# A head's four maximum blocks at 0.5 of a plan position, in place of 0.65 and 0.64

## The chip, the cores and the metric

The kernel runs on one core of one Trainium2 chip. The metric is the device time of one execution in microseconds, the median of the runs shown. Beside it stands one execution under the hardware profiler; all rows of the profile come from that one.

The engines are PE (TensorE, the matmuls), PEld (its weight loads), DVE (VectorE), ACT (ScalarE), POOL (GpSimd) and SP (SyncE, which issues transfers). Each engine works through its own instructions in the order in which the program lists them.

## What is computed

The reference is a trunk of two layers on 512 tokens of width 1024. One layer is, cut to what matters:

```python
h = rms_norm(x, attn_norm_g[l])
proj = h @ w_in[l]
c_q, c_kv, k_rope, gq, gk, gv, pool_in, gate_logits = split_columns(proj, IN_SIZES)
o_mla = mla_branch(c_q, c_kv, k_rope, ...)      # 8 heads, q and k 96 wide, v 64
o_gqa = gqa_branch(gq, gk, gv, ...)             # 8 heads on 2 k/v heads, 64 wide
o_pool = pool_branch(pool_in, ...)
merged = sum of sigmoid(gate) * (o @ w_branch) over the three branches
x = x + merged @ w_out[l]
x = x + (silu(u_gate) * u_val) @ ffn_w_down[l]  # u: conv of rms_norm(x) @ ffn_w_up
```

Both attentions are full softmax attentions over the 512 tokens:

```python
sc = jnp.einsum('bqgrd,bkgd->bgrqk', qi, k) * scale
p = jax.nn.softmax(sc, axis=-1)
```

## The kernel before

**Precision.** Every float32 operand of a matmul is split into a high and a low part, and a product is three matmuls (`mm3`, L534). A unit of weight work, as it is called here, is usually one such triple: 128 by 128 weights against 512 tokens.

**Order of a layer.** The input projection comes first, then the gqa attention, then the mla attention, then the output projection and the MLP. While an attention runs, PE has other work too: the gates of a branch (`feat_major` with the normalised input `HH`, `HL`) and the projections of the branches. They come as units from a `Filler` (L185), a generator that is stepped between the attention's steps. Beside gqa stand the units of the pool branch, the mla projections and the first of the gqa branch; beside mla the rest of the gqa branch and the first of the mla branch.

**One head of an attention** (`attention`, L1275). The head's keys and queries are turned and split (`t_q`, `t_k`, and `go_turn` for the trip through device memory that turns them). Then, step by step:

- `s_max(h, b)`, four times (b = 0 to 3; L1358): one matmul writes a block of 128 queries by 512 keys into the bank `ps_S`; DVE takes the negative maximum of each query into a column of `nm` (L314 in the profile). `ps_S` has one buffer, so the next block's matmul has to come after the reduction of the one before it. After the fourth block a transfer issued on ACT's queue (`row`, L1372) writes the 512 maxima as one row into the head's queries, `qb` in gqa and `qa` in mla.
- `probs(h, k)`, four times (L1379): 128 keys by 512 queries of scores into `ps_ST` or `ps_mi`. The row is one more line of the contraction, so that the maxima are already taken off. Then ACT takes the exponential, ACT or DVE makes the high part `ph`, DVE the low part `pl`, and a last step gathers `vt`.
- `av_hi`, `av_lo` (four each) and `av_rest`: the products with the values, in `ps_AV`.

**The plan.** The order of all these steps is made when the program is written out. Each step gets a position; a head is four positions, and head h starts at 4(h - 1). From `PLAN` come, in this order, the offsets of the turn, of `t_q`, of `t_k`, of the first `s_max`, the distance between two `s_max` blocks, the offsets of `av_hi` and `av_lo`, and the position at which the units shall be used up:

```python
tt, tq, tk, s0, ds, ah, al, end = PLAN[kind]
for h in range(8):
    p0 = 4.0 * (h - 1)
    ...
    for k in range(4):
        plan += [(p0 + s0 + ds * k, s_max, (h, k)), (p0 + 4 + k, probs, (h, k)),
                 (p0 + 4 + k + ah, av_hi, (h, k)), (p0 + 4 + k + al, av_lo, (h, k))]
```

The steps are sorted by position (a tie keeps the order of the list). Before each step, units are issued until their share fits the position:

```python
fill.upto(min(target, fill.total - spare))
while fill.done < min(target + SLACK, fill.total - spare) and waiting(fn, *args) and fill.step():
    pass
fn(*args)
```

`target` grows evenly with the position; positions below zero count PRO = 0.47 of their distance (`stretch`). `waiting` asks a clock (`Clock`, L208, and `Engine`, L279) that is advanced with assumed costs as instructions are listed: whether the step's inputs are ready and a bank is free. As long as they are not, up to SLACK = 35 units are issued ahead of their share. Among the assumed costs are 0.07 + 0.00105 us an element for a DVE reduction, 0.15 us for a signal between engines (SEM), and D_ROW = 3.4 us from the fourth reduction until the row of maxima has landed. `pick` (L506) uses the same clock to give a subtraction to DVE or POOL. The clock only sets the order: on the chip each engine goes on as soon as its semaphores allow.

Of the kernel before, what the change touches and what calls it, by code (L numbers as in the profile page):

```python
# [49 lines left out]
END = object()  # L50
RSQRT_BITS = 1597463007.0
SLACK = 35
PLAN = {"gqa": (-4.2, -1.0, -0.2, 0.0, 0.65, 2.411, 4.57, 32.003),
        "mla": (-6.2, -2.9, -1.0, 0.1, 0.64, 1.678, 1.82, 35.5)}

D_ROW, D_OUT, D_IN, D_LAT = 3.4, 3.2, 4.0, 6.0
D_SUM, D_FIRST = 2.0, (2.4, 2.4, 2.0, 2.4)
# [280 lines left out]
def trunk(ctx: ExitStack, tc: tile.TileContext, x, w, prm, gb, cst, out):  # L338
# [344 lines left out]
    def layer(l, sq, xsrc):  # L683
# [591 lines left out]
        def attention(kind, fill, okey, odst):  # L1275
# [218 lines left out]
            plan = []  # L1494
            tt, tq, tk, s0, ds, ah, al, end = PLAN[kind]
            for h in range(8):
# [514 lines left out]
```

## Time and profile before

| | us |
|---|---|
| median of 3 runs | 1546.02 |
| lowest, highest | 1543.15, 1547.62 |
| profiled execution | 1545.53 |
| its span, first to last instruction | 1543.7 |

| engine | busy us | share of the span |
|---|---|---|
| PE | 1536.6 | 100% |
| PEld | 1342.3 | 87% |
| DVE | 1171.0 | 76% |
| ACT | 1072.6 | 69% |
| POOL | 771.0 | 50% |

The first blocks of `ps_S` for gqa run at about 107 us and those for mla at about 237; in the second layer they run at 873 and 1003. A row of the profile gives a line of the kernel, an engine, an operation, the tiles as written<-read, the shape, and a count; in a list of groups the busy time and the mean duration in ns follow, in a timeline the start and the duration in us, with the idle time of the engine before it in brackets and what ended it. A tile's answer gives durations as minimum/median/maximum in ns, and the waits in us with their number.

### The profile page before, as it was taken

How to read it: one execution, taken by the hardware profiler on the slowest of the kernel's cores; microseconds unless marked ns; L12 is line 12 of the kernel's file. 1: busy time of each engine (PE TensorE's matmuls, PEld its weight loads, DVE VectorE, ACT ScalarE, POOL GpSimd, SP SyncE). 2: the span in 40 equal slices, each digit the busy share in tenths (PEclk: the TensorE clock that was granted, in tenths of full speed). 3: DMA queues.
4: the chain of work that ended last, by engine and by line, in shares of the span. 5: the costliest groups of instructions: out<-in, count | busy, mean ns of one | idle time of the engine just before them, and what ended most of it. 6: DMA issues, size and time to landing. Idle time of an engine off the chain costs nothing.

```text
span 1543.7 us, 24550 instructions
## 1 busy us (share of the span) xinstructions
PE 1536.6 (100%) x8337; PEld 1342.3 (87%) x8337; DVE 1171.0 (76%) x1960; ACT 1072.6 (69%) x2008; POOL 771.0 (50%) x828
## 2 busy tenths in 40 slices
PE   9999999999999999999999999999999999999999
PEld 8888888888889999999898888878888899999997
DVE  6877886776688888888756688768666888888885
ACT  5557875877677877786544587758766677777772
POOL 3984887753452222232488648766535522222222
PEclk9999999999999999999999999999999999999999
DMA  5432344658978888877435323546599778788763
GB/s 204 121 122 83 85 127 141 161 130 199 223 186 194 182 184 186 191 173 161 138 116 138 118 75 87 133 133 169 123 214 222 188 182 192 178 187 193 177 140 109
DMA packets 139517, 241.79 MB, mean 157 GB/s; under 512 B 30976, under 2 KB 53504, under 8 KB 139392
## 3 DMA queue, kind: packets, MB, share of 16 engines
q1 hardware_dynamic: 91872, 162.93, 33.6%
q0 software_dynamic: 42624, 77.09, 29.2%
q8 instruction: 65, 1.06, 0.3%
q10 hardware_dynamic: 4896, 0.21, 0.2%
q14 instruction: 60, 0.49, 0.1%
HBM read 149.41 MB, written 13.63 MB: 106 GB/s over the span
## 4 chain that ended last, share of the span: by engine, by line
PE 96%; DVE 2%; DMA 1%; ACT 0%; issue 0%; SPq 0%; ACTq 0%
PE ps_acc L526 41%; PE ps_AV L526 18%; PE ps_ST L526 16%; PE ps_S L526 10%; PE ps_mi L526 10%; DVE sq L306 1%; DMA qa<-nm 0%; DMA XM<-x 0%; DMA qb<-nm 0%; DVE ctl L310 0%; DVE rp L306 0%; ACT wh L299 0%; DVE gqr L306 0%; DVE ssr L314 0%; DVE ka L322 0%
## 5 line engine op out<-in xcount | busy, mean ns | idle before, releaser
L438 POOL DMA_DIRECT2D wl<-raw x188 | 170.3, 911 | 384.9 <-ACT wl L299 185.7
L299 ACT ACTIVATE wh<-raw 128x512 fp32r<-128x512 f32 (+2 forms) x449 | 264.9, 605 | 59.2 <-DVE raw L306 14.7
L306 POOL TENSOR_TENSOR wl<-raw,wh 128x512 fp32r<-128x512 f32 (+2 forms) x169 | 214.5, 1278 | 166.5 <-ACT wh L299 159.2
L438 POOL DMA_DIRECT2D fl<-raw x108 | 94.7, 876 | 166.8 <-ACT fl L299 68.6
L526 PE MATMUL ps_acc<-HH,wh 128*128 128x512 f32 x400 | 156.7, 392 | 0.4 <-DVE XM L310 0.4
L526 PE MATMUL ps_acc<-HH,wl 128*128 128x512 f32 x400 | 156.3, 391 | 0.0
L526 PE MATMUL ps_acc<-HL,wh 128*128 128x512 f32 x400 | 156.3, 391 | 0.0
L310 DVE SCALAR_TENSOR_TENSOR a<-u,prm,a 128x511 f32<-128x511 f32 x176 | 134.6, 768 | 18.9 <-ACT a L299 18.4
L314 DVE TENSOR_REDUCE nm<-ps_S 128x1 fp32r<-128x512 f32 x128 | 87.9, 686 | 46.3 <-PE ps_S L526 45.1
L299 ACT ACTIVATE wl<-wh 128x512 fp32r<-128x512 f32 (+1 forms) x188 | 118.1, 628 | 6.0
L299 ACT ACTIVATE a<-u,prm 128x512 f32<-128x512 f32 x88 | 71.2, 811 | 55.8 <-DVE u L306 55.7
L526 PE MATMUL ps_acc<-tf,wh 128*128 128x256 f32 x576 | 106.2, 282 | 0.0
L526 PEld LDWEIGHTS ps_acc<-tf,wh 128*128 128x128 f32 x576 | 94.3, 191 | 6.0
L526 PEld LDWEIGHTS ps_acc<-HH,wl 128*128 128x128 f32 x400 | 75.1, 188 | 16.3
L526 PEld LDWEIGHTS ps_acc<-HH,wh 128*128 128x128 f32 x400 | 75.3, 188 | 15.5 <-issue 0.7
L526 PEld LDWEIGHTS ps_acc<-HL,wh 128*128 128x128 f32 x400 | 75.2, 188 | 15.4
L526 PE MATMUL ps_acc<-tf,wl 128*128 128x256 f32 x288 | 81.5, 283 | 0.0
L306 DVE TENSOR_TENSOR wl<-raw,wh 128x512 fp32r<-128x512 f32 (+1 forms) x93 | 66.1, 711 | 17.6 <-ACT wh L299 17.3
L526 PE MATMUL ps_AV<-HH,wl 128*128 128x256 f32 (+1 forms) x240 | 78.2, 326 | 0.0
L526 PE MATMUL ps_AV<-HL,wh 128*128 128x256 f32 (+1 forms) x240 | 78.1, 326 | 0.0
L526 PE MATMUL ps_AV<-HH,wh 128*128 128x256 f32 (+1 forms) x240 | 78.1, 326 | 0.0
L306 DVE TENSOR_TENSOR pl<-ps_ST,ph 128x512 fp32r<-128x512 f32 x86 | 58.4, 683 | 17.1 <-ACT ph L299 13.6
(427 smaller groups left out, 5039.8 us busy)
## 6 DMA issues: line engine op xcount, KB each, us to landing
raw<-w SPq DMA_DIRECT2D x153, 512.0 KB, 4.0
wl<-raw POOLq DMA_DIRECT2D x184, 256.0 KB, 4.2
raw<-w SPq DMA_DIRECT2D x151, 256.0 KB, 3.7
fl<-raw POOLq DMA_DIRECT2D x108, 256.0 KB, 4.9
raw<-w SPq DMA_DIRECT2D x13, 384.0 KB, 3.0
XM<-x SPq DMA_DIRECT2D x16, 256.0 KB, 4.7
dtq<-tr SPq DMA_DIRECT2D x16, 192.0 KB, 2.0
dtk<-tr SPq DMA_DIRECT2D x16, 192.0 KB, 3.2
```

Of the source, the lines that this page charges most:

```text
L299: return self.eng.activation(out, in_, func, **k)
L306: return self.eng.tensor_tensor(out, *a)
L310: return self.eng.scalar_tensor_tensor(out, *a)
L314: return self.eng.tensor_reduce(out, in_, *a, **k)
L438: nc.gpsimd.dma_start(f(lo), r, accum_op=ALU.add)
L526: PE.matmul(o, lhsT=lhsT, rhs=rhs, start=start, stop=stop, skip_group_check=again)
```

## The change

The distance between two `s_max` blocks of a head becomes 0.5 positions in both attentions. Nothing else differs in the text of the kernel. The blocks b = 1, 2, 3 stand at 0.5, 1.0 and 1.5 positions behind the first in place of 0.65, 1.3 and 1.95 (gqa) and 0.64, 1.28 and 1.92 (mla). In gqa the third block of a head then has the position of the second `probs` of the head before it, and stands behind it.

```diff
 SLACK = 35
-PLAN = {"gqa": (-4.2, -1.0, -0.2, 0.0, 0.65, 2.411, 4.57, 32.003),
-        "mla": (-6.2, -2.9, -1.0, 0.1, 0.64, 1.678, 1.82, 35.5)}
+PLAN = {"gqa": (-4.2, -1.0, -0.2, 0.0, 0.5, 2.411, 4.57, 32.003),
+        "mla": (-6.2, -2.9, -1.0, 0.1, 0.5, 1.678, 1.82, 35.5)}
```

## The prediction

> **What bounds the kernel now.** I read the page's first part, its chain, and then the busy time in the four stretches in which the two attentions of the two layers run.
>
> ```profile
> span 1543.7 us, 24550 instructions
> PE 1536.6 (100%) x8337; PEld 1342.3 (87%) x8337; DVE 1171.0 (76%) x1960; ACT 1072.6 (69%) x2008; POOL 771.0 (50%) x828
> ...
> PE 96%; DVE 2%; DMA 1%; ACT 0%; issue 0%; SPq 0%; ACTq 0%
> ...
> 100.00:232.00 132.00, 132.00 (x604) 110.37 (x603) 101.58 (x186) 98.17 (x185) 92.36 (x117) 1.00 0.36 102
> 232.00:355.00 123.00, 123.00 (x536) 102.01 (x534) 89.22 (x146) 89.15 (x160) 77.93 (x76) 1.00 0.54 142
> 866.00:1000.00 134.00, 133.93 (x612) 111.98 (x611) 103.42 (x189) 100.04 (x188) 91.24 (x116) 1.00 0.35 98
> 1000.00:1124.00 124.00, 122.64 (x533) 101.30 (x532) 88.26 (x144) 88.88 (x160) 77.62 (x76) 1.00 0.56 142
> ```
>
> The reader is to see that PE has work all the time, in the attentions too (the columns are PE, PEld, DVE, ACT, POOL busy, then the clock, 1.00 throughout). In both gqa stretches DVE has 77% (101.58 of 132, 103.42 of 134), in both mla stretches 71 to 73%, so DVE is next. The change removes no matmul. What it can win is therefore only time in which PE waits, and what it can lose is new waits of PE. Busy time hides short waits, because a matmul's recorded end overlaps the next one's start; they are seen in the distance from start to start. That distance, undisturbed, is 5.44/24 = 0.227 us:
>
> ```profile
> 388.26 5.44 PE ps_ST L526 x24
> ```
>
> **The maxima, as they run now.** Two answers: the tile `nm`, and who waited for whom.
>
> ```profile
> L314 DVE TENSOR_REDUCE nm<-ps_S x128: 671/691/693, 108.2 to 1106.3; 128x1 fp32r<-128x512 f32 x128
> L1373 ACTq DMA_DIRECT2D qb<-nm x16: 476/477/554, 114.1 to 975.1; - x16
> L1373 ACTq DMA_DIRECT2D qa<-nm x16: 476/477/505, 245.5 to 1107.6; - x16
> ...
>   PEld ps_mi L526: 1.8, 1
> ...
>   PEld ps_ST L526: 0.9, 3
> ...
> DMA to landing us min/median/max: 1.9/1.9/5.8
> ...
> DVE nm L314 <- PE ps_S L526: 45.1, 57, 2.1
> ...
> PEld ps_S L526 <- POOL qa L306: 0.9, 3, 0.3
> ...
> PEld ps_S L526 <- DVE nm L314: 0.5, 2, 0.3
> ```
>
> There are 128 blocks of scores in `ps_S` (4 a head, 8 heads, 2 attentions, 2 layers), each with one matmul and one reduction of about 0.69 us, and 32 rows. PE's waits for a row are 1.8 + 0.9 = 2.7 us in the whole run. Most of it is one row, that of mla's first head in the second layer:
>
> ```profile
> 1011.79 5.81 DMA qa<-nm
> ...
> 1017.65 0.50 PE ps_mi L526
> ```
>
> It takes 5.81 us where the median is 1.9, and the scores that need it start when it lands. Of the 128 reductions 57 found DVE idle and waited for PE; the other 71 found DVE at work. That is the line that matters below, as `ps_S` has one bank: the next block's matmul cannot start before the reduction has read the bank.
>
> **What the edit moves.** A head is four positions of the plan. Its length in time, from the first scores of head 0 to those of head 7:
>
> ```profile
> 118.69 0.39 PE L526 MATMUL ps_ST<-qa,ka 128*128 128x512 f32 x1
> ...
> 212.56 0.39 PE L526 MATMUL ps_ST<-qa,ka 128*128 128x512 f32 x1
> ...
> 249.34 0.40 PE L526 MATMUL ps_mi<-qa,kl 96*128 96x512 f32 x1
> ...
> 343.58 0.40 PE L526 MATMUL ps_ST<-qa,kl 96*128 96x512 f32 x1
> ```
>
> (212.56 - 118.69)/7 = 13.41 us a head in gqa, 3.35 a position; (343.58 - 249.34)/7 = 13.46 in mla, 3.37 a position. Blocks 1, 2 and 3 of every head move up: in gqa by 0.15, 0.30 and 0.45 positions, in mla by 0.14, 0.28 and 0.42. So 96 matmuls, 96 reductions on DVE and 32 row transfers on ACT's queue stand sooner, the row by up to 0.45 x 3.35 = 1.5 us (mla 1.4; about half in head 0, whose positions are shrunk by PRO). Nothing is added or removed. They pass units of weight work (three matmuls each, 3 x 0.227 = 0.68 us) and some `av` matmuls on PE, evacuations on DVE, and exponentials and casts on ACT. No SP or POOL instruction belongs to the step. The matmuls cost nothing in another place. The row's issue takes 0.48 us on ACT's queue as before; if its reduction is late, the exponentials behind it wait, but ACT has 98.17 busy of 132, so I charge zero, and up to 0.7 (one reduction) a row if that room is gone.
>
> **Term 1, the row.** Between 0 and -2.7 us. The planner does not let the first scores stand at a fixed time: it fills with units until its clock has the row landed (D_ROW, 3.4 us after the reduction). The trace shows it: the first row leaves at 114.1 and its scores start at 118.69, 4.6 us later, though a row lands after 1.9. A sooner row takes its scores along, and a row that needs 5.81 us is then as late as before. So I take -1.0, nearer to zero.
>
> **Term 2, the bank.** At 0.65 and 0.64 positions blocks stood 2.2 us apart nominally, at 0.5 they stand 1.68. An undisturbed turn of the bank is seen here:
>
> ```profile
> 320.08 0.39 PE L526 MATMUL ps_S<-kh,qa 96*128 96x512 f32 x1
> ...
> 320.51 0.69 DVE L314 TENSOR_REDUCE nm<-ps_S 128x1 fp32r<-128x512 f32 x1 [1.67 <-PE ps_S L526]
> ...
> 321.27 0.31 PEld L526 LDWEIGHTS ps_S<-kh,qa 96*128 96x128 f32 x1
> ...
> 321.51 0.39 PE L526 MATMUL ps_S<-kh,qa 96*128 96x512 f32 x1
> ...
> 322.90 0.40 PE L526 MATMUL ps_S<-kh,qa 96*128 96x512 f32 x1
> ```
>
> 0.43 us to the reduction's start, 0.69 for it, and a load of 0.31 ahead of the next matmul: a turn of 1.39 (321.51 to 322.90) fits with nothing lost. The nominal room goes from 2.2 - 1.39 = 0.8 to 0.29 us. A late turn looks like this:
>
> ```profile
> 163.92 0.68 DVE L314 TENSOR_REDUCE nm<-ps_S 128x1 fp32r<-128x512 f32 x1
> ...
> 164.40 0.39 PE L526 MATMUL ps_acc<-oph,wl 128*128 128x512 f32 x1
> 164.65 0.31 PEld L526 LDWEIGHTS ps_S<-ka,qa 128*128 128x128 f32 x1 [0.29 <-DVE nm L314]
> 164.65 0.62 PE L526 MATMUL ps_S<-ka,qa 128*128 128x512 f32 x1
> 165.11 0.39 PE L526 MATMUL ps_AV<-ph,vg 128*128 128x512 f32 x1
> ```
>
> The reduction ends at 164.60, the load starts only then, and the two steps from 164.40 to 165.11 take 0.71 where 2 x 0.227 = 0.45 would do: 0.26 us lost, nearly all of it the load that is no longer beside another matmul. How many become late? 71 of 128 reductions find DVE at work; three quarters of them have a block of their own head behind them, 53. What they wait for is about 0.69 us long, so if they come at any moment in it, (0.69 - 0.29)/0.69 = 58% wait longer than the new room, 31 blocks, and none longer than the old 0.8. The price lies between 0 (the planner puts a unit between wherever its clock sees the bank taken) and 31 x 0.26 = 8.1 us. I take three quarters, 6.1: its clock assumes 0.07 + 0.00105 x 512 = 0.61 us for a reduction that takes 0.69, and a lateness that it does not see is not filled.
>
> [...]
>
> **Term 3, DVE in the stretch of the four blocks.** The four reductions, 4 x 0.69 = 2.76 us, fall into 1.5 positions (5.0 us) and no longer into 1.95 (6.5). The rest of DVE's work in gqa is (101.58 - 32 x 0.69)/132 = 0.60 of the time. Together 2.76/5.0 + 0.60 = 1.15 of the stretch, before 2.76/6.5 + 0.60 = 1.02. That is 0.15 x 5.0 - 0.02 x 6.5 = 0.6 us a head by which `pl` and `vt` of the head before come later, 20 us of lateness over 32 heads, from 0 to that at PE. Units stand between nearly all of them; I take a twentieth, +1.0.
>
> **Sum.** The profiled execution took 1545.53 us (span 1543.7 and 1.8 around it), 0.5 under the median of 1546.02. -1.0 + 6.1 + 1.0 = +6.1, so 1551.6 for it and 1552.1 on the median's scale; I say **1552.0**. About 0.3%, 4.6 us, is what a measurement can tell from no change: faster ends at 1541.4, slower begins at 1550.7.
>
> **Rivals.**
>
> *The planner covers it.* For it: the three blocks at 320 to 323 stand 1.43 and 1.39 us apart and PE loses nothing, and only 0.5 us of the whole run is a load that waits for a reduction. The order is made by a clock that knows the bank and DVE's queue; closer blocks then only exchange places with units. Against it: the 0.9 and 0.5 us at `ps_S` are there in spite of that clock. Term 2 falls to a tenth, 0.6, term 3 to 0.5: 1546.02 - 1.0 + 1.1 = 1546.1, with 1544 to 1550 around it. It includes the case that the change does not do what it says: where the bank and DVE hold the blocks back the row leaves no sooner, and nothing moves at all. Chance 0.36.
>
> *The load goes ahead.* If a block's load were done before the bank is free, a late block would lose only 0.02 us (164.65 - 164.40 - 0.227): 31 x 0.02 = 0.6 for term 2, +0.6 in all with the other two, 1546.6. One row speaks against it, the load at 164.65. Chance 0.04. [...]
>
> *The sooner row wins.* The other side: all 2.7 us of row waits go, because the row leaves ahead of the transfers that made it 5.81 us long, and with later, roomier scores the 0.9 + 0.5 at `ps_S` go too. 1546.02 - 4.1 = 1541.9, and it needs half a microsecond more in other waits to count as faster. It decides if rows land in 1.9 everywhere and bank turns stay free. There is hardly more to win in these stretches. Chance 0.05.
>
> *Units run out.* Sooner blocks of the heads whose `qa` comes late from POOL (the 0.9 us; POOL has 92.36 of 132) and a bank that is taken both make the planner spend units early, and then the last scores of an attention stand without any. What such a block costs its engines:
>
> ```profile
> L299 ACT ACTIVATE ps_ST<-ps_ST x22: 568/582/592, 119.4 to 218.8; 128x512 f32<-128x512 f32 x22
> L306 DVE TENSOR_TENSOR pl<-ps_ST,ph x22: 653/682/693, 121.0 to 220.6; 128x512 fp32r<-128x512 f32 x22
> L299 ACT ACTIVATE ph<-ps_ST x17: 576/598/602, 120.0 to 219.8; 128x512 fp32r<-128x512 f32 x17
> L310 DVE SCALAR_TENSOR_TENSOR vt<-ps_ST,vg,vt x15: 662/742/755, 124.5 to 219.0; 128x512 fp32r<-128x512 f32 x15
> ```
>
> 1.42 us of DVE (0.682 + 0.742), 1.18 of ACT, against four matmuls, 0.91 us, on PE: 0.5 us lost a block, 8 blocks in each of four attentions, 16 us at most, half of it likely, on top of the forecast's 1552: 1560. Against it: 35 units may be spent ahead, and now none of the four ends lacks them. Chance 0.10.
>
> **Numbers.** Forecast 0.45, alone 1550.7 to 1556 (18 blocks at 0.26 are 4.7 us over the median; all 31 are 8.1, with 1 or 2 more of term 3). Slower: 0.45 + 0.10 = 0.55; within: 0.36 + 0.04 = 0.40; faster 0.05. The range for 8 in 10, 1544.5 to 1560, leaves out the faster case, the lowest part of the covered one and half of the case of units run out.
>
> **What would show it.** Right: loads of `ps_S` that wait for the reduction go from 0.5 us to several, and steps of PE at `ps_S` of 0.46 appear in heads 0 to 3 and in mla; mla's first row leaves before 245.5. Term 1 is wrong if the row's 1.8 us goes; term 2 if loads of `ps_S` still wait under 2 us in all; term 3 if loads and matmuls of `ps_AV` wait for `pl` or `vt` by more than 2 us. The forecast is wrong if PE's distances at `ps_S` stay at 0.23 and the time within 4.6 us of 1546.0.

## The result, and the profile after

| | before | after |
|---|---|---|
| median us (6 runs each) | 1545.74 | 1552.86 |
| lowest, highest | 1543.15, 1547.62 | 1551.48, 1554.81 |
| profiled execution us | 1545.53 | 1554.81 |

The change is slower: the ratio of after to before is 1.0053, with a 95% interval of 1.0043 to 1.0063, and the medians lie 7.1 us apart. The profiled execution of after is the slowest of its runs. Its page, the parts that answer to those shown of before:

```profile
PE 1540.7 (99%) x8337; PEld 1344.1 (87%) x8337; DVE 1164.9 (75%) x1946; ACT 1082.7 (70%) x2024; POOL 769.7 (50%) x826
...
PE 88%; DMA 3%; issue 3%; DVE 2%; POOL 1%; ACT 1%; SPq 1%; POOLq 0%; ACTq 0%; DVEq 0%
```

PE has the same 8337 matmuls, but the chain of work that ended last now leaves PE for 12% of the span, before for 4%. To find the place, take the start of the first `ps_S` block of each attention, from the timelines, first before, then after:

```profile
107.43 0.39 PE L526 MATMUL ps_S<-ka,qa 128*128 128x512 f32 x1
...
236.75 0.39 PE L526 MATMUL ps_S<-kh,qa 96*128 96x512 f32 x1
...
873.50 0.39 PE L526 MATMUL ps_S<-ka,qa 128*128 128x512 f32 x1
...
1003.06 0.39 PE L526 MATMUL ps_S<-kh,qa 96*128 96x512 f32 x1
```

```profile
106.92 0.39 PE L526 MATMUL ps_S<-ka,qa 128*128 128x512 f32 x1
...
239.11 0.39 PE L526 MATMUL ps_S<-kh,qa 96*128 96x512 f32 x1
...
876.23 0.39 PE L526 MATMUL ps_S<-ka,qa 128*128 128x512 f32 x1
...
1008.63 0.39 PE L526 MATMUL ps_S<-kh,qa 96*128 96x512 f32 x1
```

From gqa's first block to mla's first block PE works through the same 585 matmuls. That stretch took 129.32 us and takes 132.19 in the first layer, 129.56 and 132.40 in the second: +2.87 and +2.84, 5.7 us in all. What PE waits for now:

```profile
PE ps_ST L526 <- DMA fl<-raw: 2.2, 2, 1.9
PE ps_S L526 <- DVE nm L314: 1.7, 4, 0.6
PE ps_ST L526 <- DVE vt L310: 1.5, 2, 0.7
...
PE ps_ST L526 <- DMA wl<-raw: 1.0, 1, 1.0
```

The second and third line, four waits for a reduction and two for `vt`, are new. All six lie at head 7 of gqa. The two lines with `raw` are weight transfers in the last MLP; they get an experiment of their own. Head 7 of the first layer before, from the timeline of PE: its third and fourth block, and the scores that need its row.

```profile
205.37 0.39 PE L526 MATMUL ps_S<-ka,qa 128*128 128x512 f32 x1
...
207.45 0.40 PE L526 MATMUL ps_S<-ka,qa 128*128 128x512 f32 x1
...
212.82 0.50 PE L526 MATMUL ps_ST<-qb,kb 65*128 65x512 f32 x1
```

Between the two blocks stand two matmuls with the values and two units, six `ps_acc` matmuls. The same head after, with the weight loads that matter below:

```profile
208.25 0.39 PE L526 MATMUL ps_ST<-qb,kb 65*128 65x512 f32 x1
...
208.94 0.31 PEld L526 LDWEIGHTS ps_S<-ka,qa 128*128 128x128 f32 x1 [0.73 <-DVE nm L314]
208.94 0.63 PE L526 MATMUL ps_S<-ka,qa 128*128 128x512 f32 x1 [0.30 <-DVE nm L314]
209.41 0.40 PE L526 MATMUL ps_AV<-ph,vg 128*128 128x512 f32 x1
210.35 0.62 PE L526 MATMUL ps_S<-ka,qa 128*128 128x512 f32 x1 [0.55 <-DVE nm L314]
210.82 0.39 PE L526 MATMUL ps_AV<-pl,vg 128*128 128x512 f32 x1
...
213.65 0.19 PEld L526 LDWEIGHTS ps_ST<-qb,kb 65*128 65x128 f32 x1 [0.55 <-DMA qb<-nm]
213.65 0.50 PE L526 MATMUL ps_ST<-qb,kb 65*128 65x512 f32 x1
...
215.31 0.50 PE L526 MATMUL ps_AV<-ph,vg 128*128 128x512 f32 x1 [0.21 <-ACT ph L299]
...
216.78 0.50 PE L526 MATMUL ps_ST<-qa,ka 128*128 128x512 f32 x1 [0.74 <-DVE vt L310]
```

There is no `ps_acc` row: between 207.55 and 217.36 PE has no unit of weight work at all. What a step takes beyond 0.227 us is lost. At the third and fourth block (208.94 and 210.35) that is 0.46 + 0.24 + 0.71 + 0.24 = 1.65 us. Behind them it is 0.28 + 0.11 us at the scores that need the row, 0.38 + 0.11 at a high part `ph` that ACT makes, and 0.90 + 0.11 at DVE's `vt`, 1.9 in all. At head 7 before, the blocks lost nothing and the scores that need the row 0.14 us (0.34 in the second layer). The heads ahead of head 7 don't lose more than they did; of the 3.55 us the stretch shows 2.87, as it had small losses of its own before, 0.14 at head 7 and more than now at the heads ahead.

Why are the units gone? The number of units that gqa's plan has left when it places the fourth block of each head (without the eight that SPARE holds back for head 7's values), counted in the order as written out:

| head | 0 | 1 | 2 | 3 | 4 | 5 | 6 | 7 |
|---|---|---|---|---|---|---|---|---|
| before | 93 | 79 | 66 | 58 | 41 | 32 | 16 | 4 |
| after | 93 | 79 | 65 | 55 | 37 | 24 | 7 | 0 |

After, none is left from the second block of head 7 on. The chain of PE shows how a block spends them. Head 5, blocks 2 to 4 before, and then after:

```profile
175.47 0.35 PE ps_S L526
175.82 0.46 PE ps_mi L526 x2
176.28 0.70 PE ps_acc L526 x3
176.98 0.24 PE ps_S L526
177.22 0.46 PE ps_AV L526 x2
177.68 0.70 PE ps_acc L526 x3
178.38 0.24 PE ps_S L526
```

```profile
178.43 0.23 PE ps_S L526
178.66 0.24 PE ps_AV L526
178.90 0.46 PE ps_mi L526 x2
179.36 1.37 PE ps_acc L526 x6
180.73 0.23 PE ps_S L526
180.96 0.24 PE ps_AV L526
181.19 1.39 PE ps_acc L526 x6
182.58 0.23 PE ps_S L526
```

Before, two matmuls of the attention and one unit (x3) fill the turn of the bank ahead of block 4, which takes 1.39 us: 1.40 from block to block. After, the last block has only one `ps_AV` in front of it, because 17.5 lies ahead of the low value product at 17.57 and 17.95 lay behind it. One unit is then too little, so the planner issues two (x6), and the blocks stand 1.85 us apart: farther than before. Block 3 takes two as well, with DVE later. Counted over all four attentions, 32 of 96 pairs of neighbouring blocks stood under 1.5 us apart before and 9 after; in gqa the mean went from 1.81 to 2.04 us. In gqa the row is not sent sooner either. Head 5's row on ACT's queue, before and after:

```profile
180.37 0.48 ACTq L1373 DMA_DIRECT2D qb<-nm  x1
```

```profile
184.62 0.48 ACTq L1373 DMA_DIRECT2D qb<-nm  x1
```

### The profile page after: what moved, and what is told of

The parts are those of the page before. It is cut to its first block, busy times and chain, and to the rows that moved or that the text cites. A ratio compares the mean times of both kernels' runs of the same rounds, so it can differ in the third digit from the quotient of the medians.

```text
span 1553.0 us, 24569 instructions
## 1 busy us (share of the span) xinstructions
PE 1540.7 (99%) x8337; PEld 1344.1 (87%) x8337; DVE 1164.9 (75%) x1946; ACT 1082.7 (70%) x2024; POOL 769.7 (50%) x826
## 3 DMA queue, kind: packets, MB, share of 16 engines
q8 instruction: 65, 1.06, 0.3%
## 4 chain that ended last, share of the span: by engine, by line
PE 88%; DMA 3%; issue 3%; DVE 2%; POOL 1%; ACT 1%; SPq 1%; POOLq 0%; ACTq 0%; DVEq 0%
PE ps_acc L526 39%; PE ps_AV L526 16%; PE ps_ST L526 15%; PE ps_S L526 9%; PE ps_mi L526 9%; DMA raw<-w 1%; DMA fl<-raw 1%; DMA wl<-raw 1%; POOL wl L306 1%; DMA tf<-dtq 0%; SPq L860 0%; DVE nm L314 0%; ACT wh L299 0%; DVE ctl L310 0%; DVE win L306 0%
## 5 line engine op out<-in xcount | busy, mean ns | idle before, releaser
L306 POOL TENSOR_TENSOR wl<-raw,wh 128x512 fp32r<-128x512 f32 (+3 forms) x167 | 212.9, 1283 | 164.8 <-ACT wh L299 158.1
L299 ACT ACTIVATE ps_ST<-ps_ST 128x512 f32<-128x512 f32 x86 | 50.1, 583 | 35.3 <-PE ps_ST L526 33.4
```

What stands on the lines that cost most here:

```text
L299: return self.eng.activation(out, in_, func, **k)
L306: return self.eng.tensor_tensor(out, *a)
```

## The experiments

Theory U is this: the loss is in gqa, where closer positions make the planner spend its units too early. Theory B is the forecast's second term: close blocks turn the bank late wherever they are. All kernels were timed in five rounds against the kernel before on the same chip, except the last two. A ratio stands with its 95% interval; the microseconds beside it are its part of the median of before, and the difference of the two medians is up to 1.1 us away from them.

**Each attention alone.** The first edit takes gqa alone to 0.5, the second mla alone.

```diff
-PLAN = {"gqa": (-4.2, -1.0, -0.2, 0.0, 0.65, 2.411, 4.57, 32.003),
+PLAN = {"gqa": (-4.2, -1.0, -0.2, 0.0, 0.5, 2.411, 4.57, 32.003),
```

> Only gqa at 0.5, mla stays at 0.64. Theory U (units run out): in gqa the closer blocks have fewer other matmuls between them, so the planner spends a unit more per block and has none left from the third block of head 7 on; PE then waits about 3.5 us there in each layer. The whole loss is here: +6 to +8.5 us, and PE's long steps lie at head 7 alone. Theory B (late bank turns everywhere, the forecast's term 2): both attentions lose alike, so about half, +3 to +4 us, in steps of 0.46 us spread over all heads.

```diff
-        "mla": (-6.2, -2.9, -1.0, 0.1, 0.64, 1.678, 1.82, 35.5)}
+        "mla": (-6.2, -2.9, -1.0, 0.1, 0.5, 1.678, 1.82, 35.5)}
```

> Only mla at 0.5, gqa stays at 0.65. U: no loss, since units are left at the end of mla; the 1.5 us wait for the row of mla's first head in the second layer may go: -2 to +0.5 us. B: +3 to +4 us, with late loads of ps_S in mla.

gqa alone: 1.0045 (1.0033 to 1.0058), +6.9 us. mla alone: 1.0008 (0.9999 to 1.0017), +1.2 us, not told from zero. The first lies in U's range and above B's. The second is above U's and below B's, but its interval reaches into U's. So nearly all of the loss is gqa's, as U says and B doesn't. The waits of PE with gqa alone hold the same two new lines as after, 1.7 us for `nm` and 1.5 for `vt`. With mla alone PE's waits show none for `nm`. What is new in mla is a wait for a `ph` that DVE made, at head 3 in both layers (with mla alone there is one for `pl` beside it). The row is from the profile of the change, which has the wait for `ph` too:

```profile
288.48 0.50 PE L526 MATMUL ps_AV<-ph,vm 128*128 128x512 f32 x1 [0.30 <-DVE ph L322]
```

By steps of PE it costs 0.6 and 0.4 us in the two layers of the change. With mla at 0.64, in the kernel before and with gqa alone, PE loses nothing at that head.

**Units given back.** The next kernel is the change with eight units more beside gqa (and eight more beside mla in place of those taken away); the one after it has the same for the distances of before, as its control.

```diff
-SOONER = {1: 4 * KC, 0: 7 * KC}
+SOONER = {1: 5 * KC, 0: 8 * KC}
```

> The change as it is, with 8 units more beside gqa (and as many more taken from the next branch beside mla, so that mla keeps its number). U: units last to the end of gqa, so the time goes back to that of before, 1543 to 1547 us. B: the blocks are as close as in the change, so the time stays at 1551 to 1554 us.

> The kernel before (0.65 and 0.64) with the same 8 units more beside gqa. U: the few tenths that head 7 of gqa still waits for its row or its low parts in each layer go, and nothing else: -1.5 to +0.5 us. B: no change, within 1 us.

The change with eight more: 1.0031 (1.0020 to 1.0042), 1549.57 us, between the ranges of U and B. The waits of PE at head 7's blocks and scores are gone; the eight units bring a wait of their own, where the units of the gqa branch reach the last heads' output before it is there:

```profile
233.72 0.50 PE L526 MATMUL ps_acc<-oh,wh 128*128 128x512 f32 x1 [0.81 <-ACT oh L299]
```

The control has that wait too and stands at 1.0011 (1.0002 to 1.0020), +1.7 us, above what either theory said, though its interval reaches down to 0.3 us. So the change's 0.0053 over before shrinks to 0.0020 over its control, about 3 us. In the profiles 0.9 us of that is seen: gqa's stretches take 135.09 and 135.38 us, in the control 134.74 and 134.86, and the difference lies in small losses of heads 2 to 6. So want of units is the larger part of the loss but not shown to be all of it; the other 2 us stay open.

A smaller gift: gqa alone at 0.5, with four units more.

```diff
-SOONER = {1: 4 * KC, 0: 7 * KC}
+SOONER = {1: 4 * KC + 4, 0: 7 * KC + 4}
```

> gqa at 0.5, mla at 0.64, with 4 units more beside gqa (and 4 more of the next branch beside mla). U: units last over all blocks of head 7, so its waits at the bank (1.7 us a layer) go, those at its scores stay: +2 to +4.5 us against before, 3 to 5 below gqa alone at 0.5. B: as gqa alone at 0.5, +6 to +8 us.

1.0023 (1.0014 to 1.0032), +3.6 us, half of gqa's loss, within U's range and outside B's. No wait for `nm` at the bank is left; what is left is the row of head 7, with no unit in front of the scores that need it:

```profile
216.55 0.50 PE L526 MATMUL ps_ST<-qb,kb 65*128 65x512 f32 x1 [1.33 <-DMA qb<-nm]
```

Four of the eight reserved units, released sooner, with the number unchanged:

```diff
-SPARE = KC
+SPARE = 4
```

> gqa at 0.5, mla at 0.64, the number of units beside gqa unchanged, but of the 8 units that are held back until head 7's values 4 may be spent sooner. U (units run out): they last over the blocks of head 7, so its waits at the bank go (1.7 us a layer), and part of it returns as waits behind its scores or at its values: +2 to +6 us against before, under gqa alone at 0.5 by 1 to 4. B (close blocks turn the bank late): unchanged, +6 to +8 us.

1.0034 (1.0021 to 1.0048), +5.3 us. The bank's waits at head 7 go again, and most of it comes back behind: 1.06 for the row, 0.34 and 0.73 for `vt`.

```profile
215.71 0.50 PE L526 MATMUL ps_ST<-qb,kb 65*128 65x512 f32 x1 [1.06 <-DMA qb<-nm]
```

Head 7 still loses 2.9 and 3.1 us in the two layers, where gqa alone at 0.5 lost 3.55. The time is within U's range, but its interval, 3.2 to 7.4 us, reaches into B's; it is the trace that tells them apart. Releasing the last units sooner moves most of the waits and removes few of them; four units more took half of the loss away.

**Units taken away at the old distance.**

```diff
-SOONER = {1: 4 * KC, 0: 7 * KC}
+SOONER = {1: 3 * KC, 0: 6 * KC}
```

> The kernel before (0.65 and 0.64), with 8 units fewer beside gqa and as many fewer taken from the next branch beside mla. U: units run out at the third block of head 7 though the blocks stand as far apart as before, so PE waits there and at the scores of head 7 as in the change: +4 to +8 us. B: the distance is that of before, so 0 to +1 us.

1.0084 (1.0069 to 1.0098), +13 us, the right sign and more than U's +8. Counted as above, none is left from the second block of head 7 on, as in the change. With the blocks at their old positions, head 7 shows the waits of the change at the blocks, and a larger one for its row:

```profile
205.09 0.63 PE L526 MATMUL ps_S<-ka,qa 128*128 128x512 f32 x1 [0.83 <-DVE nm L314]
206.50 0.62 PE L526 MATMUL ps_S<-ka,qa 128*128 128x512 f32 x1 [0.32 <-DVE nm L314]
...
211.60 0.50 PE L526 MATMUL ps_ST<-qb,kb 65*128 65x512 f32 x1 [2.14 <-DMA qb<-nm]
```

By steps of PE, 4.4 us are lost there in the first layer. So the waits need no closer blocks; lack of units is enough. In the second layer 6.1 us are lost, and 1.6 of them are not waits. Behind the wait for the row (2.18 us, up to 982.45) the granted clock, the last column but two, is 0.50 for about 3.5 us, and a matmul takes 0.43 us from start to start:

```profile
983.00:984.00 1.00, 1.00 (x4) 0.81 (x3) 0.63 (x2) 0.81 (x2) 0.96 (x1) 0.50 0.00 0
```

Of the five executions four have a mean granted clock under 1, down to 0.997; the one at 1.000 took 1554.47 us, 10 above the median of before. So a part of the +13 is the clock's, which neither theory had.

**Other distances in gqa.**

```diff
-PLAN = {"gqa": (-4.2, -1.0, -0.2, 0.0, 0.65, 2.411, 4.57, 32.003),
+PLAN = {"gqa": (-4.2, -1.0, -0.2, 0.0, 0.4, 2.411, 4.57, 32.003),
```

> gqa at 0.4, closer still; mla stays at 0.64. At 0.4 the high and low value products of the head before stand together between the second and third block, so the plan spends fewer units on the blocks than at 0.5, and the last units are spent at the first scores of head 7, as at 0.65. Theory U (units run out before head 7's blocks): no wait of PE at the blocks of head 7, 0 to +3 us against before. Theory B (closeness of the blocks costs late bank turns): more than at 0.5, over +7 us.

```diff
-PLAN = {"gqa": (-4.2, -1.0, -0.2, 0.0, 0.65, 2.411, 4.57, 32.003),
+PLAN = {"gqa": (-4.2, -1.0, -0.2, 0.0, 0.55, 2.411, 4.57, 32.003),
```

> gqa at 0.55; mla stays at 0.64. U: only block 1 still stands ahead of the low value product, the units are gone from head 7's fourth block on and no longer from the third, so a part of the loss of 0.5: +4 to +6.5 us, at head 7. B: a third or more of the way back from 0.5 to 0.65, +4 to +5 us, spread over the heads. The trace tells them apart, the time does not.

At 0.4: 1.0025 (1.0015 to 1.0035), +3.9 us: less than at 0.5, against B, and more than U's +3. No block of head 7 waits for its reduction; by the count two units are left at its fourth block in the first layer and five in the second. One block of head 2 does wait for its bank (0.31 us at 135.08), as B would have it. Other instructions wait, in heads 2 to 4 of the first layer, for accumulator banks that ACT (0.26 us at 133.45) or DVE still reads, which neither theory had named:

```profile
155.50 0.39 PE L526 MATMUL ps_acc<-wh,cth 128*128 128x256 f32 x1 [0.54 <-DVE XM L310]
```

At 0.55: 1.0038 (1.0024 to 1.0052), +5.9 us. The waits are at head 7, as U says, but gqa's stretch of the first layer is 132.65 us, not shorter than the 132.13 with gqa alone at 0.5, so the trace shows no smaller loss there. The count says why: one unit is left at head 7's second block and none from the third on, not from the fourth as U had it. At 0.58 and at 0.60, where all value products keep their places between the blocks, the order written out is the one of before, instruction for instruction on every engine. So it is with 0.5 when `al` is set to 4.45, ahead of the second block. They are the program of before, so there is nothing to time. In gqa the distance by itself does nothing; what a block passes in the order does.

**The MLP's waits.** The change and the kernel before were each profiled once more, in a single execution.

> The change once more, one profile. Its first profile has 3.1 us of PE waits in the MLP of the second layer (at 1222 and 1305 us) that gqa alone at 0.5 doesn't have. If they belong to the change (theory M: the order ahead of the MLP shifts its weight transfers), they stand there again, 2.5 to 3.5 us. If they belong to that one execution (theory E), they come with another size or not at all, while the waits at head 7 of gqa, 3.5 us a layer, are the same to 0.3 us.

> The kernel before once more, one profile. Theory E: PE's waits in the MLP of the second layer, 0.2 us in its first profile, may be anything from 0 to 3 us. Theory M: 0.2 us again. Both: head 7 of gqa loses under 0.5 us a layer.

The waits of PE for weights, after and then before:

```profile
PE ps_ST L526 <- DMA wl<-raw: 1.1, 1, 1.1
PE ps_ST L526 <- DMA fl<-raw: 1.1, 1, 1.1
```

```profile
PE ps_ST L526 <- DMA fl<-raw: 1.3, 1, 1.3
PE ps_ST L526 <- DMA qa<-nm: 1.1, 1, 1.1
```

The kernel before now has 1.3 us there where its first profile had none over 0.2, and after has 2.2 where it had 3.2, under the range of M. So these waits differ from execution to execution of one program. In the first profile of after one of them (1.88 us, up to 1304.81) was followed by a granted clock of 0.50 from 1307 to 1309; in the second profile of it no such drop is seen. gqa's stretch does not differ: 132.21 and 132.37 us in the second profile of after, 129.41 and 129.48 in that of before.

## Why the prediction was right

The size and the sign were right, 1552.0 against 1552.86, and the mechanism of the largest term was wrong. That the sum fits is luck: its +6.1 was worked out from 31 late turns of the bank over all heads, and there were four, all at head 7 of gqa. They cost 3.3 us, and the scores and values of the same head cost 3.8, where the sum had 1.0 for all heads.

**Term 1, the row (-1.0).** Half right. In gqa the row does not leave sooner: the first one left 6.7 us behind gqa's first block before (114.1 - 107.43) and after (113.6 - 106.92), and head 5's 4.8 us later than before (72.9 and 77.7 us behind it). In mla it does: the first one left 8.7 us behind mla's first block (245.5 - 236.75) and now 6.7 (245.8 - 239.11). The answer for the tile after:

```profile
L1373 ACTq DMA_DIRECT2D qb<-nm x16: 476/477/548, 113.6 to 981.3; - x16
L1373 ACTq DMA_DIRECT2D qa<-nm x16: 476/477/478, 245.8 to 1105.8; - x16
```

The wait of 1.8 us for the row of mla's first head is gone after, which the prediction had named as the sign that -1.0 is wrong. That this was the change's doing is not shown: in the second profile of before that wait is gone too, and one of 1.1 us stands at head 5 of mla. With mla alone the time didn't fall.

**Term 2, the bank (+6.1).** This step failed. It turned positions into time (0.5 x 3.35 = 1.68 us) and let 31 blocks over all heads come late by 0.26. But a position is not a time here. The planner waits for the bank by issuing units, so closer positions gave wider blocks in gqa. Loads of `ps_S` that wait for the reduction did grow from 0.5 us to several, as the prediction's sign asked:

```profile
PEld ps_S L526 <- DVE nm L314: 3.4, 4, 1.0
```

But these four loads are the four late turns at head 7, two in each layer, for lack of units; in heads 0 to 6 and in mla, where the forecast had put them, there is none, and the two of before are gone. The four cost 2 x 1.65 = 3.3 us. One late turn cost 0.70 and 0.95 us, not 0.26: the exposed load, 0.24, was right, the wait ahead of it is longer without units. At 208.94 and 210.35 the load starts with its matmul, after the reduction, as in the row at 164.65 of before, and the wait stands in the load's own row. Of the 248 loads of `ps_S`, before and after, that follow another block of their attention, none started sooner than 0.05 us after that block's reduction had ended. So no run shows the 0.02 us a late turn of the rival "The load goes ahead"; the late turns lost 0.70 and 0.95.

**Term 3, DVE's lateness (+1.0).** This was right in kind and too small. It needed "units between nearly all of them", and where there were none it showed: DVE's `vt` cost 0.90 + 0.11 us a layer at head 7, 2.0 us in all. The `ph` at head 3 of mla, late with units in front of it, adds 0.6 and 0.4. The other 1.8 us at head 7's scores and values are not this term: 0.49 a layer is a `ph` of ACT's, 0.39 the wait for the row.

**The rivals.** "Units run out", held at 0.10, is what happened, in a smaller form. It was priced for eight blocks in each of four attentions, 1560; only gqa ran out, from its head 7's second block on, and lost 5.7 us. Its reason was half right: a bank that is taken spends the units early, at head 5 through one matmul fewer between the blocks, not through a late `qa` from POOL. "The planner covers it", at 0.36, holds for heads 0 to 6 and, but for head 3, for mla. The argument against the run-out, that no end of an attention lacked units before, was wrong too: gqa had four left at head 7's last block and none at its first scores, as the count shows. The row of 0.50 us at 212.82 before, with 0.03 lost ahead of it and 0.11 behind, was a sign of it.

Of the 7.1 us between the medians (8.2 by the ratio), gqa's stretches account for 5.7 in the profiled executions, and the new waits in mla for 1.0. The rest is within what the MLP's waits (1.0 us and more between two profiles of one kernel) and the clock (1.6 us with eight units fewer) change from execution to execution, and is not settled.

## What to carry to other kernels

When a program orders its work by a plan that fills waits with other work, a step's position is not its time; ask which instructions change places, and how much filling each gap needs afterwards. Filling work is a stock: count what is left of it at the end of the stage, since a small extra use at several places is paid at once where the stock ends. If a position is moved and nothing passes anything, the program is the same.

## What was not expected of the hardware

A step that waited for its bank lost its weight load as well: 0.24 us beside the wait, behind 208.94 and 210.35 after and behind 205.09 with eight units fewer. The load takes 0.31; at 178.04 after, with no wait, it ran beside the matmul ahead of its own, and both steps kept 0.23. And the landing of the 2 KB row is not a property of the program alone: in the two profiles of before its wait stood at different heads of mla, 1.4 us at head 0 and 1.1 us at head 5. Two waits of PE were followed by half the clock: after 2.18 us (eight units fewer) and 1.88 us (after) the granted clock was 0.50 for about 3 us, which cost 1.6 us in the first case; after a wait of 2.14 us in the same execution, at 211.60, it stayed at 1.00.
